# Predicting one edit: five engines made to run their instructions in the order of emission (hybrid decoder step, Trainium2)

## The chip, the core and the metric

The kernel runs on one NeuronCore of a Trainium2 chip, all of whose five engines it uses: TensorE (matmuls and transposes), VectorE, ScalarE, GpSimd and SyncE (which only issues the DMA transfers). Each engine runs its own list of instructions in the order of that list; an instruction waits for its operands at the head of the list, and the ones behind it wait with it. The metric is the device time of one execution in microseconds. Times are medians of several executions; the profile is of one more execution.

## The reference, cut to what matters

Two layers of a hybrid decoder over 1104 tokens (16 learned meta tokens and 1024 of a prompt, and 8 sequences of 8 sampled tokens), model width 1024, feed-forward width 2816. Three token mixers (gated DeltaNet with 4 heads, Mamba-2 with 4 heads, sliding-window attention with sinks) read one common input projection, and one output projection reads all three.

```python
def trunk_layer(x, pos, lw, states, front_pad, chunk, attend):
    m, new_states = hybrid_mixer(rmsnorm(x, lw['g_pre_mix']), pos, lw, states, front_pad, chunk, attend)
    x = x + rmsnorm(m, lw['g_post_mix'])
    gate, up = jnp.split(rmsnorm(x, lw['g_pre_ffn']) @ lw['w_ffn_in'], 2, axis=-1)
    x = x + rmsnorm((jax.nn.silu(gate) * up) @ lw['w_ffn_out'], lw['g_post_ffn'])
    return x, new_states
```

Inside the DeltaNet mixer a state is carried from block to block of the sequence, so its steps are a chain that can't be cut:

```python
    def step(s, inp):
        u_c, w_c, attn_c, qd_c, kd_c, gl_c = inp
        v_new = u_c - jnp.einsum('bhcd,bhde->bhce', w_c, s)
        o_c = jnp.einsum('bhcd,bhde->bhce', qd_c, s) + jnp.einsum('bhij,bhje->bhie', attn_c, v_new)
        s = s * gl_c[..., None, None] + jnp.einsum('bhcd,bhce->bhde', kd_c, v_new)
        return s, o_c
```

## The kernel before, in words

Tiles. The 1104 tokens are nine tiles of 128 tokens (the last has 80; `NT`, `tsz`). For full precision every weight slab comes from memory as float32 (`raw`) and is split into a high and a low float16 half (`wsp`): a ScalarE activation makes the high half, a VectorE `scalar_tensor_tensor` the low half. The activations are split in the same way (`xn`, `mixed`, `hsp`). A product is three float16 matmuls, accumulated in PSUM.

Stages of a layer. (1) Norm and transposition of the tokens into `xn`; input projections, attention, and the gates. (2) The DeltaNet and Mamba columns of the input projection, each followed by its short convolution (`conv_post`, tiles `R` and `u`), the preparation of each block of 128 tokens (`dn_inv`, `dn_prep`) and the chain over the blocks (`dn_chain`: `ps_ch`, `r`, `y`, `S`). (3) The output projection, from `mixed` into PSUM `pd`, then per tile the post-norm, the residual sum `xt`, the next norm and the transposes of `m` (`out_post`, line 2026). For the last three tiles (`NPT`) the part of the first three heads is computed early and parked in DRAM. (4) The feed-forward's input projection into `hid` and `hsp`, in a form with seven products in place of eight (`FSEQ`, `combos`, `hid_sums`). (5) The feed-forward's output projection with the post-norm `ffn_post`, which also makes the next layer's `xn`.

Who sets the order. The source is a set of generators (`dense`, `loader`, `dn_chain`, `out_post` and others), each of which emits some instructions and then yields a condition. The class `Plan` (line 116) chooses which goes on: it keeps a clock for each engine (`clk`, for T, V, S, G, D: TensorE, VectorE, ScalarE, GpSimd and the DMA queue of SyncE), adds the modelled duration of every emitted instruction (`note`, with `HOP` and `RATE`), and takes the generator of the lowest priority number that can go on without TensorE waiting. Its result is one list of instructions, in order of emission. All engine calls go through `Plan.engine` (line 206); its inner call stands at line 214, which is why every row of the profile bears L214, and rows are told apart by tile names.

The list of emission isn't yet the order on the engines. The framework's tile scheduler takes it, knows every data dependency, and puts each engine's instructions into an order by its own estimate of when each is ready; of several that are ready the first emitted goes first. So an instruction emitted later can stand ahead of one emitted earlier on the same engine, if the earlier one isn't expected to be ready. That order is fixed when the kernel is built.

Places that the steps below touch. The head of the program (lines 2108 to 2132) emits the loads in the order: first token tile, constants, gains, weight slabs 0 and 1, second token tile, slab 2, third token tile, slab 3; `first_load` (line 541) emits each slab's split at once, and all four stand before the first tile's square on ScalarE. In `dense` the output projection of a tile waits for all its inputs at once:

```python
                yield (tuple(("mix", l, h, i) for h in range(4)) + (("ssm", l, i), ("swa", l, i))
                       + tuple(wo if i == 0 else ()))
```

and after the nine tiles comes `yield (("ffn", l),)`, before the first feed-forward matmul is emitted. The buffers: 23 large ones in rotation (`NG`), two for raw slabs, three for split slabs, two PSUM banks for `pd` and six more for the short matmuls (`ps_tr`, `ps_inv`, `ps_ch`, `ps_o`).

Of the kernel before, what the change touches and what calls it, by code (L numbers as in the profile page):

```python
# [110 lines left out]

NG = 23
NOW = -1.0


class Plan:
# [38 lines left out]
    def note(self, k, name, out, ins, acc, slow=False):  # L155
# [40 lines left out]
        if k != "D" or out.space != DRAM:  # L196
# [6 lines left out]
                L.append(b + (e + self.HOP[k],))  # L203
            self.last = max(self.last, e + self.HOP[k])

    def engine(self, eng, k):
        plan = self

        class E:
            def __getattr__(self, name):  # L210
                f = getattr(eng, name)

                def call(*a, **kw):
                    r = f(*a, **kw)  # L214
                    aps = [x for x in list(a) + [v for n, v in kw.items() if n not in ("out", "accum_out")]
                           if isinstance(x, bass.AP)]
                    out = kw.get("out")
                    if out is None:
                        out, aps = aps[0], aps[1:]
                    plan.note(k, name, out, aps, [kw["accum_out"]] if "accum_out" in kw else [],  # L220
                              kw.get("op") is ALU.pow)
                    return r

                return call

        return E()

    def mark(self, *keys):
        for key in keys:
            self.done[key] = self.last  # L230
# [5 lines left out]
    def run(self, *until):  # L236

        done = self.done
        while not until or any(k not in done for k in until):
# [31 lines left out]
            best[1], best[2] = self.last, None  # L271
            if r == NOW:
                best[1] = 0.0
# [8 lines left out]
def build(tc, A, depth=DEPTH):  # L282
    nc = tc.nc
    P = Plan()
    V, S, G, T, DQ = (P.engine(e, k) for e, k in ((nc.vector, "V"), (nc.scalar, "S"), (nc.gpsimd, "G"),
                                                 (nc.tensor, "T"), (nc.sync, "D")))
    dma = DQ.dma_start
    mark, done = P.mark, P.done
    es = ExitStack()
# [8 lines left out]
    def act(out, in_, func=AF.Copy, **k):  # L298
        S.activation(out=out, in_=in_, func=func, **k)
# [4 lines left out]
    def tt(out, a, b, op):  # L304

        n = 1
        for x in out.shape[1:]:
            n *= x
        t = {k: max(P.clk[k], P.clk["T"]) + P.RATE[k][0] * n for k in "VG"}
        (V if t["V"] <= t["G"] else G).tensor_tensor(out, a, b, op=op)  # L310
# [42 lines left out]
    def PS(tag):  # L353
        n = {"tr": 1, "inv": 2, "ch": 1, "o": 2}[tag]
        t = psm.tile([128, 512], F32, tag=tag, bufs=n, name="ps_" + tag)
        P.take(tag, n, t)
        return t
# [31 lines left out]
    def later(key, fn, n=0):  # L389

        def g():
            yield (key,)
            fn()
            free(n)
            mark((key, "st"))
        P.add(0, g())

# [13 lines left out]
    def load7(my, key, src):  # L411
# [11 lines left out]
        for k in range(4):  # L423
# [5 lines left out]
            def put(o, x):  # L429
                yield P.clk["V"]  # L430
                act(w[:, o, :512], x, scale=WS)
                stt(w[:, o, 512:], x, WS, w[:, o, :512], MUL, SUB)
# [20 lines left out]
            mark(key + (k,))  # L453
            yield NOW

# [6 lines left out]
    def loader():  # L462
        while True:
# [31 lines left out]
            if key[0] == "w2" and key[2] == 0:  # L495
# [3 lines left out]
                split[0] += 1  # L499
                yield NOW  # L500
                continue
# [29 lines left out]
            mark(key)  # L531
            yield NOW

# [52 lines left out]
    def norm_t(xt, C, i, gb, dst, xs, tag, halves=False):  # L586
# [6 lines left out]
        for hf in range(2):  # L593
# [13 lines left out]
            V.tensor_tensor(lo, pc, hi, op=SUB)  # L607
            yield NOW if hf == 0 else None

# [19 lines left out]
    def dense_ws(p, w, xn, g):  # L629

        g0, gn = g
        for kt in range(8):
            mm3(p[:, :gn], w[:, 0, kt * 128:(kt + 1) * 128], w[:, 1, kt * 128:(kt + 1) * 128],
                xn[:, kt, 0, g0:g0 + gn], xn[:, kt, 1, g0:g0 + gn], kt == 0, kt == 7)
            if kt < 7:
                yield NOW

# [1622 lines left out]
def make(arrays, depth=DEPTH):  # L2260
    import concourse.bacc as bacc

    nc = bacc.Bacc("TRN2", target_bir_lowering=False, num_devices=1)
    A = {n: nc.dram_tensor(n, a.shape, mybir.dt.from_np(a.dtype), kind="ExternalInput").ap()
         for n, a in arrays.items()}
    for n, s in OUTS.items():
        A[n] = nc.dram_tensor(n, s, F32, kind="ExternalOutput").ap()
    with tile.TileContext(nc) as tc:
        build(tc, A, depth)
    return nc  # L2270
# [9 lines left out]
```

## Time and profile before

| | us |
|---|---|
| median of 3 executions | 2900.02 |
| lowest, highest | 2899.88, 2901.44 |
| the profiled execution | 2895.58 |
| its span in the trace | 2893.5 |

Mean granted clock of TensorE in the profiled execution: 0.981 of full speed. The rows of the views stand in a section of their own below. How to read them: times are microseconds; PE is TensorE's matmuls, PEld its weight loads, DVE is VectorE, ACT ScalarE, POOL GpSimd, SP SyncE. In a timeline each row is a run of like instructions: start, busy time, engine, operation, output<-input tiles, and how many; the bracket gives how long the engine stood idle just before and what ended that. Matmuls are pipelined, so their records overlap by some tenths of a microsecond.

### The profile page before, as it was taken

To read this page: it belongs to the slowest core of one execution; us is meant where nothing else is said; L and a number is where in the kernel's file an instruction comes from. 1 tells how busy PE (TensorE), PEld (TensorE's weight loads), DVE (VectorE), ACT (ScalarE), POOL (GpSimd) and SP (SyncE) were. 2 spreads that over 40 slices of the span, in tenths; PEclk is the share of its full clock that TensorE was granted. 3 is DMA by queue.
4 is the path that set the end of the run, shared out by engine and by line. 5 is a ranking of instruction groups with operands and counts; after the bars stand their busy time and mean duration, and the time that the engine had idled before them with its cause. 6 is when DMAs were issued, how large, how long until landed. Compare 5 with 4: busy or idle time off the path is not lost. (4 is left out here: it accounts for less than half of the span.)

```text
span 2893.5 us, 50019 instructions
## 1 busy us (share of the span) xinstructions
PE 2743.2 (95%) x19662; PEld 1909.5 (66%) x19662; DVE 1933.3 (67%) x3614; ACT 1288.4 (45%) x3015; POOL 813.1 (28%) x1124
## 2 busy tenths in 40 slices
PE   6999999999799999999899999999998999999997
PEld 3766677664588888744348676777646888886443
DVE  5557667655757676767865676666457666766776
ACT  5435456554423333433544455655543333334342
POOL 2204523313543333200260062223136233231011
PEclk8999999999899999999999999999999999999998
DMA  5011110132301111242431111001222111113333
GB/s 183 31 60 37 57 38 31 38 104 89 109 30 59 53 51 59 96 120 68 163 128 34 50 47 46 31 31 56 86 103 87 50 54 59 52 52 110 106 115 124
DMA packets 74092, 209.79 MB, mean 73 GB/s; under 512 B 13360, under 2 KB 24816, under 8 KB 73824
## 3 DMA queue, kind: packets, MB, share of 16 engines
q1 hardware_dynamic: 73856, 206.59, 21.8%
q8 instruction: 154, 2.52, 0.4%
q14 instruction: 82, 0.67, 0.1%
HBM read 175.49 MB, written 33.04 MB: 72 GB/s over the span
## 5 line engine op out<-in xcount | busy, mean ns | idle before, releaser
L214 PEld LDWEIGHTS <-wsp 128*128 128x128 f16 x10704 | 1044.1, 99 | 305.7 <-issue 12.9
L214 PE MATMUL pd<-xn,wsp 128*128 128x336 f16 (+3 forms) x4512 | 737.7, 311 | 3.4 <-DVE a L214 3.1
L214 DVE SCALAR_TENSOR_TENSOR wsp<-raw,wsp 128x512 f16<-128x512 f32 (+2 forms) x414 | 404.8, 986 | 196.3 <-ACT wsp L214 193.5
L214 ACT ACTIVATE wsp<-raw 128x512 f16<-128x512 f32 (+2 forms) x414 | 311.0, 763 | 393.5 <-DVE raw L214 145.9
L214 PEld LDWEIGHTS <-hsp 128*128 128x128 f16 x1848 | 182.1, 99 | 242.0 <-issue 30.2
L214 PE MATMUL pd<-wsp,hsp 128*128 128x512 f16 x924 | 232.6, 385 | 17.1 <-ACT wsp L214 11.8
L214 PE MATMUL ps_o<-wsp,hsp 128*128 128x512 f16 x924 | 230.7, 383 | 0.5 <-DVE m L214 0.5
L214 PE MATMUL pd<-wsp,mixed 128*128 128x512 f16 (+1 forms) x864 | 212.0, 384 | 5.8 <-DVE m L214 5.8
L214 POOL TENSOR_SCALAR rqy<-ss 128x1 f32<-128x1 f32 (+1 forms) x72 | 56.1, 779 | 551.1 <-ACT jk L214 407.6
L214 DVE SCALAR_TENSOR_TENSOR u<-R,lp_cw,u 128x512 f32<-128x512 f32 x216 | 180.0, 869 | 4.3 <-ACT u L214 3.4
L214 ACT ACTIVATE hsp<-hid 128x512 f16<-128x512 f32 x154 | 89.8, 620 | 180.4 <-PE ps_o L214 143.7
L214 PE MATMUL pd<-wsp,xn 128*128 128x512 f16 (+3 forms) x864 | 161.2, 338 | 6.0 <-ACT wsp L214 3.4
L214 PE MATMUL ps_o<-xn,wsp 128*128 128x256 f16 (+1 forms) x1296 | 165.1, 285 | 0.0
L214 POOL TENSOR_TENSOR raw<-raw 128x512 f32<-128x512 f32 x74 | 95.5, 1292 | 241.9 <-DVE raw L214 208.4
L214 PE MATMUL ps_inv<-xn,wsp 128*128 128x256 f16 (+1 forms) x1248 | 154.0, 281 | 0.8 <-DVE a L214 0.8
L214 POOL TENSOR_TENSOR U<-U,hid 128x256 f32<-128x256 f32 (+1 forms) x114 | 80.3, 733 | 239.3 <-ACT hid L214 239.3
L214 PEld LDWEIGHTS <-mixed 128*128 128x128 f16 (+1 forms) x864 | 84.4, 101 | 82.4 <-issue 11.3
L214 DVE TENSOR_TENSOR hsp<-hid,hsp 128x512 f16<-128x512 f32 x154 | 101.4, 684 | 43.3 <-ACT hsp L214 43.3
L214 PEld LDWEIGHTS <-xn 128*128 128x128 f16 (+1 forms) x864 | 87.4, 103 | 55.9 <-issue 10.7
L214 PE MATMUL ps_ch<-xn,wsp 128*128 128x296 f16 x456 | 109.2, 289 | 0.0
L214 PE MATMUL ps_tr<-xn,wsp 128*128 128x256 f16 x456 | 108.6, 273 | 0.0
L214 DVE TENSOR_TENSOR W<-ps_inv,c 128x512 f16<-128x512 f32 (+1 forms) x120 | 71.0, 595 | 46.3 <-PE ps_inv L214 45.4
(496 smaller groups left out, 4738.9 us busy)
## 6 DMA issues: line engine op xcount, KB each, us to landing
raw<-wfi SPq DMA_DIRECT2D x88, 512.0 KB, 3.5
raw<-wfo SPq DMA_DIRECT2D x70, 512.0 KB, 3.7
raw<-wf SPq DMA_DIRECT2D x44, 512.0 KB, 3.3
xd<-xt SPq DMA_DIRECT2D x24, 512.0 KB, 2.9
xt<-xd SPq DMA_DIRECT2D x24, 512.0 KB, 5.7
xt<-x SPq DMA_DIRECT2D x16, 512.0 KB, 6.1
raw<-wo SPq DMA_DIRECT2D x16, 512.0 KB, 3.4
tcx<-wfo SPq DMA_DIRECT2D x10, 512.0 KB, 3.7
```

The lines of the kernel that those rows point to most:

```text
L214: r = f(*a, **kw)
```

## The change

Every instruction on the five engines gets an ordering edge to the instruction emitted before it on the same engine. The edge is for the tile scheduler alone: it says "not ahead of that one" and adds no wait for that one's end. Nothing is added to the work, taken from it or given another shape; which buffer of a rotation an instruction uses, and for whom it waits, can differ as the order does.

```diff
+PINNED = "TVSGD"
...
+    def keep(self, k, ins):
+
+        return self.pin(ins) if k in PINNED else ins
...
                 def call(*a, **kw):
-                    r = f(*a, **kw)
+                    r = plan.keep(k, f(*a, **kw))
...
     P = Plan()
+    P.pin = tc.keep_in_program_order
```

## Rows read from the trace of the kernel before

**Rows 1.** Top of the page: the span, then busy time (share, instructions) of each engine.
```profile
span 2893.5 us, 50019 instructions
...
PE 2743.2 (95%) x19662; PEld 1909.5 (66%) x19662; DVE 1933.3 (67%) x3614; ACT 1288.4 (45%) x3015; POOL 813.1 (28%) x1124
```

**Rows 2.** Table by stage: stretch, its length, busy time of engines, clock, DMA share, GB/s.
```profile
core 0: us, PE busy (x) PEld busy (x) DVE busy (x) ACT busy (x) POOL busy (x), PEclk, DMA share, GB/s
0.00:61.40 61.40, 41.15 (x212) 22.61 (x212) 32.41 (x55) 31.38 (x68) 16.16 (x35) 0.92 0.54 186
...
240.00:640.00 400.00, 377.80 (x2992) 278.57 (x2990) 268.83 (x565) 229.03 (x597) 138.09 (x208) 0.99 0.15 50
640.00:684.00 44.00, 41.08 (x259) 25.92 (x257) 19.79 (x57) 18.30 (x66) 11.18 (x18) 1.00 0.18 60
...
752.00:791.00 39.00, 29.72 (x222) 24.04 (x221) 31.93 (x35) 15.98 (x30) 25.19 (x26) 0.85 0.36 119
791.00:1390.00 599.00, 598.90 (x4406) 433.30 (x4405) 416.25 (x767) 221.67 (x457) 144.71 (x176) 1.00 0.22 69
1390.00:1470.00 80.00, 67.92 (x314) 30.93 (x313) 70.40 (x82) 40.26 (x66) 23.19 (x26) 0.96 0.56 179
...
1660.00:2064.00 404.00, 382.04 (x3021) 281.75 (x3020) 271.48 (x569) 230.66 (x599) 138.07 (x208) 0.99 0.15 50
...
2815.00:2893.00 78.00, 57.83 (x245) 24.75 (x243) 56.42 (x65) 23.38 (x36) 15.06 (x12) 0.89 0.38 129
```

**Rows 3.** Waits of TensorE, 240 to 640: waiting tile <- releaser, sum, times, longest.
```profile
PE ps_ch L214 <- ACT qs L214: 6.7, 3, 3.2
PE ps_ch L214 <- DVE lt L214: 3.9, 2, 2.0
```

**Rows 4.** Timeline of all engines, 502 to 513, without the weight loads.
```profile
503.22 2.00 PE L214 MATMUL ps_ch<-Sb,kq 128*128 128x128 f32 x16
...
505.69 3.62 DVE L214 SCALAR_TENSOR_TENSOR u<-R,lp_cw,u 128x616 f32<-128x616 f32 x3
...
509.23 0.33 DVE L214 SCALAR_TENSOR_TENSOR r<-ps_ch,nE,prep 64x128 f32<-64x128 f32 x1
...
509.93 0.39 PE L214 MATMUL ps_ch<-S,ck 128*16 128x128 f32 x2 [3.20 <-ACT qs L214]
```

**Rows 5.** The end of the chain, 646.5 to 683.5, all instructions (columns as rows 2).
```profile
646.50:683.50 37.00, 34.08 (x207) 21.53 (x206) 16.29 (x49) 15.24 (x57) 10.27 (x15) 1.00 0.19 64
```

**Rows 6.** The same stretch, instructions on `pd` alone: PE, DVE, ACT busy.
```profile
646.50:683.50 37.00, 15.97 (x56) 0.00 (x0) 1.83 (x4) 1.00 0.19 64
```

**Rows 7.** Timeline of TensorE, 745 to 791.
```profile
744.62 2.10 PE L214 MATMUL pd<-wsp,mixed 128*128 128x512 f16 x9
748.85 0.63 PE L214 MATMUL ps_tr<-c,m 128*128 128x128 f32 x4 [2.12 <-DVE m L214]
...
752.01 1.75 PE L214 MATMUL ps_o<-xn,wsp 128*128 128x256 f16 x8
...
760.42 3.19 PE L214 MATMUL ps_o<-xn,wsp 128*128 128x256 f16 x14
763.41 0.75 PE L214 MATMUL ps_tr<-c,m 128*128 128x128 f32 x4
```

**Rows 8.** Timeline of all engines, 750 to 771: steps of the norm chains.
```profile
755.06 3.36 DVE L214 SCALAR_TENSOR_TENSOR xt<-m,rqy,xt 128x1024 f32<-128x1024 f32 x1 [2.10 <-POOL rqy L214]
...
760.90 1.06 ACT L214 ACTIVATE xn<-xt 128x1024 f16<-128x1024 f32 x1
760.94 0.55 POOL L214 TENSOR_TENSOR rqy<-rqy,mhalf 128x1 f32<-128x1 f32 x1
...
761.52 1.28 DVE L214 SCALAR_TENSOR_TENSOR m<-xt,rqy,gpf 128x1024 f32<-128x1024 f32 x1 [0.72 <-POOL rqy L214]
```

**Rows 9.** Timeline of VectorE, 1396 to 1412: one of the products.
```profile
1400.35 1.22 DVE L214 TENSOR_TENSOR m<-m,gb 128x1024 f32<-128x1024 f32 x1
```

**Rows 10.** Timeline of ScalarE, 0 to 45: the fourth weight split.
```profile
23.37 1.06 ACT L214 ACTIVATE wsp<-raw 128x1024 f16<-128x1024 f32 x1
```

**Rows 11.** Timeline of TensorE, 0 to 45: its first instructions.
```profile
8.48 1.11 PE L214 MATMUL ps_tr<-c,xt 128*128 128x128 f32 x4 [8.48 <-DVE xt L214]
```

## The prediction, made before the changed kernel was built

> **What bounds the kernel now.** I read the page first. TensorE is busy in 2743.2 of the 2893.5 us, so at most 150 us of the span can be saved by any order, and any loss must show as new idle time on that engine [rows 1]. The table by stage says where the 150 us lie [rows 2]. One stretch of the feed-forward input projection fills TensorE: 598.90 of 599.00 us. The idle time sits at the head (61.40 against 41.15), in the token mixers of each layer (400.00 against 377.80, so 22.2 us), at the end of the DeltaNet chain (44.00 against 41.08), between out-projection and feed-forward (39.00 against 29.72, so 9.3 us), in the feed-forward's output (80.00 against 67.92, with VectorE busy 70.40) and in the tail. The second layer repeats the first, one row of it stands for that. So the change is priced by these stages. In the mixers I then read the waits of TensorE [rows 3]: it stands mostly before the short matmuls of the DeltaNet chain, which need a ScalarE or VectorE result.
>
> **What the change does to an engine.** No instruction is added or removed. Both kernels issue on each engine in one fixed order; before, a scheduler chose it and let ready work overtake, after, it is the order of emission, which the planner chose. The instructions carry the number of their emission. Outside the longest run in order stand 964 of the 18,392 matmuls, 1,234 of the 3,614 VectorE, 614 of the 2,759 ScalarE, 214 of the 1,121 GpSimd and 97 of the 487 SyncE instructions; most are within 200 numbers of their place. An overtaker either filled a hole or made something more urgent late. Pinning gives back the second kind and loses the first. I took each stage for itself.
>
> **Mixers, gain.** The rows show the second kind. A matmul group into `ps_ch` ends at 505.22. The VectorE step `r` that reads it runs at 509.23, behind three convolution steps of 3.62 us in all; the next chain matmul starts at 509.93 after 3.20 us of idle TensorE [rows 4]. In the source the `r` is emitted before those three. I followed the larger gaps of the 22.2 us back in the same way, and in some nine tenths of that time the releasing step had been ready behind a later-emitted one. I take three quarters as given back, 15 us, as an estimate. Against it: convolutions that were early will now be late, and the in-order ScalarE and VectorE wait for each other; 8 us of new idle time, an estimate from about a third of what stands there today. Net -7 us a layer, bounds -18 and +15.
>
> **Chain end, loss.** In 646.5 to 683.5 the chain of the last head runs, and the only other work for TensorE is the out-projection of tiles 0 to 5, for the heads that are done. The scheduler moved 54 of these matmuls (`pd<-wsp,mixed`) into the holes of the chain: of 34.08 us of TensorE time in 37.00, they are 15.97 as the profile counts overlapping records [rows 5, 6]. In the source `dense` waits for all four heads of a tile, and in the emission these matmuls all come after the chain. Their real price is the pipelined rate, 2.10 us for 9, 0.23 us each [rows 7]: 54 x 0.23 = 12.5 us that move behind the chain. The chain, freed of them, should be some 2 us shorter. Net +10 us a layer, bounds +4 (chain quicker by half of them) and +13.
>
> **Out-projection to feed-forward.** Here feed-forward matmuls (`ps_o<-xn,wsp`, at 752.01 and 760.42 for 1.75 and 3.19 us) run before the transposes `ps_tr<-c,m` of the last tiles at 763.41 [rows 7]. In the source, nine tiles' out-projection and all nine norms come first. TensorE then waits out the norm chain of a tile: eviction, square on ScalarE 1.06 (plus its accumulator), reciprocal root on GpSimd, `xt` on VectorE, square 1.06, root 0.55 and its step before, `m` 1.28 [rows 8]. That is 7 to 8 us, and up to 9 where `xt` meets GpSimd's product, as its 3.36 us do. Walking the emission by hand with these durations I get two stalls of 7.5 and 8.4 us and 2.3 us of small ones, 18.2 instead of 9.3. Before 752 the strict order saves some 4 us, among them the 2.12 us at 748.85 [rows 7], whose norm was overtaken. Net +5 a layer, bounds -3 and +12.
>
> **Feed-forward output.** VectorE is nearly full there. Now the products `m<-m,gb` of 1.22 us stand between the steps that split the weights [rows 9]; in the source they come later, which gives time back. But a split is a ScalarE step and then a VectorE step, and in strict order VectorE waits where it used to take something else. I take +3 a layer, bounds -5 and +15 (two bubbles of about a microsecond for each of the slab pairs).
>
> **Head.** ScalarE's fourth weight split runs at 23.37 today, and TensorE starts at 8.48 [rows 10, 11]. In the source the four splits stand before the first tile's square, so TensorE starts when the fourth slab has landed and a norm is done: about 23, an estimate from the issue of these transfers moving up a few microseconds. The 41.15 us of work up to 61.40 [rows 2] then end near 65 if nothing else is late: +4, bounds -2 and +12.
>
> **At nothing.** Feed-forward input: TensorE has no idle time to lose, but every one of the queues could stall it; VectorE is at 416.25 of 599.00 [rows 2], which leaves cover. Bound +6 a layer. SyncE: DMA share is 0.15 to 0.22 in the long stages [rows 2], so a transfer that is issued some places later is covered; without that cover a slab would stall TensorE by its landing, so I keep +-3. Sum: 2 x (-7 + 10 + 5 + 3) + 4 = +26 us. The profiled run took 2895.58 us, 2.1 more than its span and 4.4 under the median; so 2921.6 for such a run and 2926 for the median.
>
> **A clock rule.** TensorE's granted clock is 1.00 at the chain end and 0.85 in the stretch after it that has the stalls [rows 2]. The second means that part of it ran at 1.2 instead of 2.4 GHz, after idle time. If the chain end without its fillers fell to that 0.85, and the next 39 us to 0.75, the cost would be 37 x 0.15 + 39 x 0.10 = 9.5 us a layer, 19 in all: 2945. The Trainium skill, "TensorE: Matmul & The Clock Gate", section "What's actually happening", says that the engine's default is the halved clock and that only recent activity lifts it. By that rule the loss is larger than the moved matmuls alone; the 0.85 agrees, and no row shows the chain end without fillers. I count it as a rival.
>
> **Rivals.** (1) Faster: overtaking on VectorE is what makes the idle time. Place: the mixers' chain steps. If these stalls go to under 5 us a layer (-18), the chain end costs only 5, out-projection evens out, feed-forward output gives 2 and the head 2, the sum is 2 x -15 - 2 = -32: 2868. For it: rows 4 repeat all over the mixers. Against it: the holes at chain end are shown. It decides if the mixers gain over 16 us a layer. Chance 0.31. (2) The halved clock, 2945, chance 0.10. (3) New waits everywhere: putting today's matmuls into source order and leaving their producers' ends where they are gives 144 us more idle time (worked out over all 19,662 records [rows 1]), of which at most 85 were delayed by overtaken producers. If a half of that is not recovered the loss is about 100: 3000. Chance 0.08. (4) The gains of the mixers (-13) and the losses (+8, +5) cancel: 2900, chance 0.11.
>
> **How the numbers follow.** The forecast, slower by 6 to 60 us, has 0.40. Under and over 0.2%, 6 us, is what a measurement of this kernel can tell from no change. Faster 0.31, same 0.11, slower 0.40 + 0.10 + 0.08 = 0.58. The forecast's own range is 2906 to 2955. Most of rival 1 must be inside: the range is 2868 to 2980, and it leaves out the far half of rivals 1 and 3.
>
> **What would show it.** Right: idle TensorE time before `ps_ch` in the mixers falls by half; between 646 and 684 no `pd<-wsp,mixed` stand among the chain's matmuls and TensorE is busy about half the time; two stalls of 7 to 8 us before `ps_tr<-c,m`; the first matmul after 20 us. Wrong: fillers that the planner itself emitted into the chain end, or a feed-forward input stage with more than 6 us of idle time, which would be a queue that I held to be covered.

## The result and the profile after

The changed kernel takes 3025.09 us (median of 4 executions, 3023.55 to 3028.07), the one before 2899.95 in the same series: 1.0434 times as long, 95% interval 1.0421 to 1.0447. That is 125 us more where +26 was forecast, and above the range, whose upper end was 2980.

The top of the page after, as in rows 1:

```profile
span 3022.1 us, 49957 instructions
...
PE 2780.8 (92%) x19662; PEld 1938.9 (64%) x19662; DVE 1972.1 (65%) x3614; ACT 1282.4 (42%) x3015; POOL 812.4 (27%) x1124
```

The same 19,662 matmul records now take 37.6 us more of TensorE's time, and the span is 128.6 us longer; so 91 us are new idle time, and 38 us are the same work taking longer, at a mean granted clock of 0.958 where it had 0.981. The table by stage of the kernel after shows both (columns as in rows 2, the first number after the stretch and its length being TensorE's busy time; the stretches are about those of rows 2, found again by emission numbers, and so lie elsewhere on the time axis):

```profile
229.00:601.00 372.00, 350.35 (x2746) 265.77 (x2745) 254.95 (x549) 209.90 (x553) 140.92 (x204) 0.96 0.12 42
...
640.00:687.30 47.30, 33.89 (x154) 23.64 (x154) 18.55 (x55) 15.42 (x57) 10.11 (x15) 0.73 0.14 44
...
759.70:817.50 57.80, 35.18 (x232) 27.47 (x232) 42.39 (x52) 23.66 (x43) 30.85 (x33) 0.76 0.34 110
817.50:1425.00 607.50, 599.46 (x4406) 433.15 (x4404) 420.48 (x749) 208.63 (x443) 141.20 (x169) 1.00 0.21 67
1425.00:1535.00 110.00, 86.03 (x376) 38.92 (x374) 84.48 (x96) 49.33 (x80) 21.44 (x35) 0.91 0.42 141
```

The chain end (second line) has lost its fillers: the granted clock is 0.73, a mean of stretches at 2.4 and at 1.2 GHz, where rows 2 have 1.00. The stretch of the last tiles' norms (third line) has 22.6 us of idle TensorE in 57.8. The feed-forward output (last line) is 110 us long, with VectorE busy 77% of it; rows 2, over its densest 80 us, have 88%.

The numbers of emission are the same in both kernels, so a ledger can be made: for each stage, the end of the last matmul whose number lies below the stage's last one, minus the same for the stage ahead. Each column is one execution. The runs on which the argument rests are in it; of others that leave the source's order alone, single stages are quoted below (us; layer 1, then layer 2; "V" is VectorE, "T" TensorE, "FFN" the feed-forward; the runs are told below; "V in mixers" has the pins in the head too):

| stage | before | all pinned | T alone | all but T | all but V | V in mixers | V after mixers |
|---|---|---|---|---|---|---|---|
| head and attention in | 230.3 | 219.9 | 230.6 | 220.2 | 222.1 | 234.0 | 229.9 |
| mixers, first part | 193.1 | 183.6 | 192.9 | 179.8 | 192.7 | 180.5 | 194.8 |
| mixers, second part | 222.6 | 235.3 | 242.2 | 222.8 | 239.2 | 222.4 | 223.7 |
| chain end | 37.6 | 45.6 | 44.0 | 40.3 | 47.6 | 39.1 | 41.2 |
| out-projection, first FFN columns | 137.4 | 163.5 | 159.7 | 147.4 | 163.6 | 137.8 | 146.0 |
| FFN in | 498.9 | 507.6 | 500.2 | 508.3 | 503.0 | 498.9 | 506.8 |
| FFN out | 164.6 | 186.0 | 172.4 | 185.2 | 177.8 | 164.8 | 178.4 |
| layer 2: attention in | 167.8 | 166.6 | 165.6 | 169.5 | 166.9 | 167.8 | 165.2 |
| mixers, first part | 195.4 | 184.3 | 195.2 | 181.7 | 201.5 | 182.7 | 197.1 |
| mixers, second part | 222.0 | 235.0 | 246.6 | 222.1 | 238.6 | 224.1 | 222.6 |
| chain end | 37.4 | 50.6 | 48.9 | 39.8 | 47.3 | 37.5 | 38.0 |
| out-projection | 139.5 | 166.8 | 162.5 | 161.2 | 165.9 | 139.6 | 157.4 |
| FFN in | 499.4 | 510.2 | 500.8 | 508.1 | 505.3 | 499.4 | 503.6 |
| FFN out | 136.4 | 152.9 | 139.1 | 151.9 | 144.4 | 136.1 | 149.0 |

Read it by columns: what the change gave (the head 10, the first part of the mixers 10 and 11) and what it took (13 a layer in the second part of the mixers, 8 and 13 at the chain ends, 26 and 27 in the out-projection, 9 and 11 in the feed-forward input, 21 and 17 in its output).

The waits of TensorE in the whole kernel after, longest kinds (waiting tile <- releaser, sum, times, longest):

```profile
PE ps_tr L219 <- DVE m L219: 72.8, 21, 11.1
PE pd L219 <- ACT wsp L219: 26.3, 9, 5.4
```

The first stood at 31.2 us before, the second at 15.2: the transposes behind the norms, and the weight slabs of the feed-forward output. The two stalls of the forecast's pair are seen in TensorE's timeline after:

```profile
762.21 1.46 PE L219 MATMUL pd<-wsp,mixed 128*128 128x512 f16 x6
772.40 1.09 PE L219 MATMUL ps_tr<-c,m 128*128 128x128 f32 x4 [8.73 <-DVE m L219]
...
785.43 1.09 PE L219 MATMUL ps_tr<-c,m 128*128 128x128 f32 x4 [8.53 <-DVE m L219]
```

### The profile page after: what moved, and what is told of

The parts are those of the page before. It is cut to its first block, busy times and chain, and to the rows that moved or that the text cites. A ratio compares the mean times of both kernels' runs of the same rounds, so it can differ in the third digit from the quotient of the medians.

```text
span 3022.1 us, 49957 instructions
## 1 busy us (share of the span) xinstructions
PE 2780.8 (92%) x19662; PEld 1938.9 (64%) x19662; DVE 1972.1 (65%) x3614; ACT 1282.4 (42%) x3015; POOL 812.4 (27%) x1124
## 5 line engine op out<-in xcount | busy, mean ns | idle before, releaser
L219 PE MATMUL pd<-xn,wsp 128*128 128x336 f16 (+3 forms) x4512 | 728.1, 310 | 6.6 <-ACT xn L219 3.5
L219 DVE SCALAR_TENSOR_TENSOR wsp<-raw,wsp 128x512 f16<-128x512 f32 (+2 forms) x414 | 378.0, 924 | 205.1 <-ACT wsp L219 202.9
L219 POOL TENSOR_SCALAR rqy<-ss 128x1 f32<-128x1 f32 (+1 forms) x72 | 37.5, 521 | 641.8 <-ACT jk L219 444.5
L219 PE MATMUL pd<-wsp,xn 128*128 128x512 f16 (+3 forms) x864 | 154.7, 332 | 0.0
L219 DVE SCALAR_TENSOR_TENSOR hid<-a,hid 128x256 f32<-128x256 f32 (+2 forms) x190 | 85.2, 465 | 40.6 <-ACT a L219 38.0
```

Source lines behind the costliest of these rows:

```text
L219: r = plan.keep(k, f(*a, **kw))
```

## The experiments

The theory after the result was A: what TensorE loses are matmuls that filled holes, and now stand behind what waits. The rival was B: the orders of the other engines make new waits. Differences are against the kernel before as timed with each run. Two executions of such a run lie up to 15 us apart, so I draw nothing from differences under some 8 us unless the ledger shows their place.

**1. Which engine's order: TensorE alone, all but TensorE.**

```diff
-PINNED = "TVSGD"
+PINNED = "T"        # first run
+PINNED = "VSGD"     # second run
```

> Only TensorE in the order of emission, the other four engines ordered by the scheduler as before. The changed kernel lost 125 us: by common instruction numbers -10 in the head, 0 in the mixers, +32 at the two chain ends, +58 between the out-projections and the feed-forwards (first feed-forward columns included), +50 in the feed-forward outputs. Theory A (TensorE's own order: matmuls that used to fill holes now stand behind what waits): chain ends and out-projections lose the same here, 32 + 58, the outputs little: 2985, 2960 to 3010. Theory B (the other engines' orders make the new waits): 2900 to 2930.

> TensorE ordered by the scheduler, the other four in the order of emission. Theory A: the matmuls fill the holes at the chain ends and out-projections again, the outputs of the feed-forward stay slow (waits on ScalarE's and VectorE's weight splits): 2940, 2915 to 2965. Theory B: 3000 to 3025, nearly all of the loss stays.

Measured: 3018.0 (+124) with TensorE alone, outside both answers, and 2957.6 (+64) with all but TensorE, inside A's range (2915 to 2965). TensorE's order alone costs as much as all five, and the other four without it half as much. The two don't add up to 125, so the losses share places. The ledger parts them. TensorE's own order costs the second part of the mixers (+20 and +25), the chain ends and most of the out-projection's loss (22 and 23 of 26 and 27). The other four orders give the head and the mixers their gain, and cost the feed-forward: its input 9 us a layer, its output 21 and 16. They also cost the out-projection 10 and 22 without TensorE's. So A and B are both there, mostly each in stages of its own, and in the out-projection either is enough for much of the loss.

**2. The DMA queue free.**

```diff
-PINNED = "TVSGD"
+PINNED = "TVSG"
```

> As the changed kernel, but SyncE's DMA queue is ordered by the scheduler. If loads that stand behind stores in the queue delay the norm chains (the store of a token tile waits for its last step, the next tile's load is issued after it), 10 to 25 us come back: 3000 to 3015. If the loads are early enough anyway, nothing moves: 3025 within 6.

Measured: 3014.3 (+121). By the time itself that lies just inside the first answer, by the difference (+121 against +125) it is the second: nothing moves. The ledger has 4 us less in each feed-forward output, and 9 more in the head, where TensorE's first matmul comes at 28.41 in place of 19.47. The queue's order is no term of the loss.

**3. VectorE free.**

```diff
-PINNED = "TVSGD"
+PINNED = "TSGD"
```

> As the changed kernel, but VectorE is ordered by the scheduler. The theory says that overtaking on VectorE was what cost the first half of the mixers and what filled the bubbles of the feed-forward output. So mixers: the gain of 10 us a layer goes, +20; feed-forward input and output: 10 + 20 us a layer come back, -55; sum 2990. If the stages don't hang on VectorE but on ScalarE's or the queue's order, the mixers keep their gain and the outputs stay slow: 3015 to 3030.

Measured: 3031.5 (+132), outside the first answer and just above the second. The total hides that the mechanism did show: the mixers' gain goes (192.7 and 201.5, where all pinned gives 183.6 and 184.3), and the feed-forward gets back 5 a layer in its input and 8 in its output. What I had wrong is the size of the second part: TensorE, still pinned, holds the rest.

**4. VectorE's order alone, in one place at a time.** Here the pins are switched with the stage, and only VectorE has them (`PINNED = "V"`):

```diff
+    on = True              # in the second run False
...
-        return self.pin(ins) if k in PINNED else ins
+        return self.pin(ins) if self.on and k in PINNED else ins
...
             mark(("gains", l))
+            P.on = False       # second run: True
...
         sub.close()
+        P.on = True            # second run: False
         sub = ExitStack()
         L.ssp = pool("ssm", 1, stack=sub)
```

> VectorE alone in the order of emission, and only where the faster mixed version has its pins (head, first layer's attention, mixers of both layers); every other engine ordered by the scheduler. If overtaking on VectorE is what the mixers lost, their 10 to 12 us a layer come here too, the head's gain (which went where the DMA queue was free) does not: 2876 to 2882. If it takes all four orders, 2890 to 2900.

> VectorE alone in the order of emission, and only from the out-projection to the end of the next layer's attention (out-projection, feed-forward in and out); every other engine ordered by the scheduler. With TensorE free and the other four pinned these stages lost 52 and 46 us. If VectorE's order makes these waits, 2950 to 2990. If they come from ScalarE's, GpSimd's or the queue's order, or only from orders that don't fit each other, 2899 to 2915.

Measured: 2872.4 (-25; ratio 0.9912, interval 0.9895 to 0.9928) with VectorE pinned in the mixers, and 2961.0 (+64; 1.0222, 1.0196 to 1.0247) with it pinned after them. The first goes a little beyond its first answer (2876 to 2882), the second lies in its first. One engine's order is thus the gain in one stage and most of the feed-forward's loss in another. In VectorE's timeline of the first of the two the step `r` of rows 4 runs when its matmul is done, and convolution steps like those that stood ahead of it come after:

```profile
499.97 0.34 DVE L220 SCALAR_TENSOR_TENSOR r<-ps_ch,nE,prep 64x128 f32<-64x128 f32 x1 [2.27 <-PE ps_ch L220]
...
505.69 0.74 DVE L220 SCALAR_TENSOR_TENSOR u<-R,lp_cw,u 128x512 f32<-128x512 f32 x1
...
508.59 0.84 DVE L220 SCALAR_TENSOR_TENSOR u<-R,lp_cw,u 128x616 f32<-128x616 f32 x1
```

and of TensorE's waits in the mixers (240 to 600) the longest kind is a quarter of the one in rows 3:

```profile
PE ps_ch L220 <- ACT qs L220: 1.7, 3, 1.1
```

In the second of the two, VectorE's timeline in the feed-forward output has a fixed pattern, which the changed kernel shows with the same times:

```profile
1420.29 1.22 DVE L220 TENSOR_TENSOR raw<-tcx,raw 128x1024 f32<-128x1024 f32 x1
1422.63 1.22 DVE L220 SCALAR_TENSOR_TENSOR wsp<-raw,wsp 128x1024 f16<-128x1024 f32 x1 [1.12 <-ACT wsp L220]
1423.77 0.68 DVE L220 TENSOR_TENSOR hsp<-hid,hsp 128x512 f16<-128x512 f32 x1
1424.37 1.22 DVE L220 TENSOR_TENSOR raw<-raw,tcx 128x1024 f32<-128x1024 f32 x1
1426.71 1.23 DVE L220 SCALAR_TENSOR_TENSOR wsp<-raw,wsp 128x1024 f16<-128x1024 f32 x1 [1.12 <-ACT wsp L220]
```

The source emits a slab's subtraction, ScalarE's half and VectorE's half back to back. In that order VectorE stands idle 1.12 us for ScalarE's half, for each slab. Before, the next slab's subtraction or a norm's product ran there [rows 9]. From late in layer 1's feed-forward input to the end of its output, VectorE's waits of this kind sum to 12.8 us in the changed kernel and to 3.5 before.

**5. Is that bubble the loss of the feed-forward output?** Two tries. One lets the planner emit other work inside the pair, everything pinned; the other takes the version with VectorE pinned after the mixers and lets two kinds of steps move ahead again.

```diff
             act(w[:, 0, :n], x, scale=WS)
+            if key[0] == "w2":
+                yield None                     # first try
             stt(w[:, 1, :n], x, WS, w[:, 0, :n], MUL, SUB)
...
+                    P.on, on = "", P.on        # second try, here and around hsp's
                     V.tensor_tensor(raw, *((x, raw) if key[2] == 7 else (raw, x)), op=SUB)
+                    P.on = on
```

> As the changed kernel, all engines in order of emission; but in the feed-forward output's weight slabs the planner may emit other work between the ScalarE half of a split and the VectorE half that needs it. If the bubbles of 1.12 us of VectorE before each second half are what makes this stage 21 and 16 us longer, most of it comes back: 2993 to 3003. If the order of the slabs against the sums of hid sets it, or the clock, 3015 to 3028.

> As the version that pins VectorE alone from the out-projection on (+64 us), but two kinds of its VectorE steps in the feed-forward output may move ahead again: the subtraction that prepares a weight slab (raw) and the low halves of hid (hsp). So one of them can run in the 1.12 us in which VectorE waits for a split's ScalarE half. If that bubble is what VectorE's order costs there, the outputs go from 178 and 149 us to 166 and 138: 2899 + 64 - 23 = 2940, 2930 to 2945. If it is the place of the norm products or the slabs' order, 2955 to 2965.

Measured: 3041.7 (+143, so 17 worse than the changed kernel) and 2951.9 (+52, 11 better than the version that it is made from, against 23 expected). VectorE in the first try:

```profile
1454.88 1.22 DVE L219 SCALAR_TENSOR_TENSOR wsp<-raw,wsp 128x1024 f16<-128x1024 f32 x1
1456.61 0.69 DVE L219 TENSOR_TENSOR hsp<-hid,hsp 128x512 f16<-128x512 f32 x1 [0.51 <-ACT hsp L219]
1460.08 1.23 DVE L219 TENSOR_TENSOR raw<-raw,tcx 128x1024 f32<-128x1024 f32 x1 [2.78 <-DMA raw<-wfo]
```

The bubble of 1.12 us is gone, and a wait of 2.4 to 3.3 us for the next slab's load has come in its place. There are two raw buffers, a load can start when a split has freed one, and in strict order what stands behind the subtraction stands with it. So the try failed by a wait that it made itself. In the second try the ledger has 173.7 and 144.3 for the outputs, with 178.4 and 149.0 where VectorE is all pinned and 164.6 and 136.4 before. Freeing these two kinds of steps thus gives back about a third of what VectorE's order costs there. That try has waits for loads of its own, so the bubble's exact share is not shown; which other steps make the rest I have not parted.

**6. Fillers at the chain end.** The planner, read out while it emits, gives the reason why they are missing. All 23 large buffers are taken from the gains' load on. `dense` can't pass its `room(2)` for the first tile until the last chain frees four, and by the planner's own clock TensorE idles 19.0 us there (the trace has 13.5, at a lower clock). In two steps I emitted a full tile's matmuls ahead of that condition; the second doesn't wait for the last head either:

```diff
             for i in range(NT):
                 C = tsz(i)
+                ps = []
+                if i not in part:
+                    yield (tuple(("mix", l, h, i) for h in range(3)) + (("ssm", l, i), ("swa", l, i))
+                           + tuple(wo if i == 0 else ()))      # first step: range(4)
+                    for hf in range(2):
+                        ps.append(pd())                        # first step: all eight slabs here
+                        yield from dense_tok(ps[hf], mx, wo[hf * 4:hf * 4 + 4], i, 512, (0, 1, 2, 4, 5, 6, 7),
+                                             last=False)
+                        yield NOW
+                    yield (("mix", l, 3, i),)
+                    for hf in range(2):
+                        yield from dense_tok(ps[hf], mx, wo[hf * 4:hf * 4 + 4], i, 512, (3,), first=False)
+                        yield NOW
                 yield room(2)
                 hold(2)
```

> As the changed kernel, all engines in order of emission; but dense emits the two halves' matmuls of a full tile's out-projection ahead of the condition room(2), the wait for two of the 23 large buffers, which the planner's own account grants only when the last head's chain is done. So the planner can emit some 48 matmuls into the chain end. If that room is what keeps the fillers out, and the halved clock comes from the missing work, the two chain ends get back most of their 32 us: 2995 to 3005. If the fillers were not the cause, or block the chain's own matmuls, 3020 to 3030.

> As the changed kernel, all engines in order of emission; but a full tile's out-projection for the first three heads and the other mixers (seven of eight slabs) is emitted without waiting for the last head or for the two buffers, the eighth slab when that head is there. So 48 of its matmuls stand among the last chain's, as many as the scheduler put there (44), where the earlier try got 30 in. If the missing fillers are the loss of this stretch, 11 us of work a layer move and the clock stays up: 2995 to 3003. If the norm chains and rooms of the tiles set the end of the out-projection whatever stands in the chain, 3015 to 3027.

Measured: 3022.8 (+129) and 3010.6 (+113). The first, as its second answer said, put 30 matmuls ahead of the chain's last step and gained nothing; the second, between its two answers, put 48 there, about as many as the scheduler, and gained about 12 us. The ledger charges 8 and 13 us to the chain ends, and the moved matmuls some 10 us a layer to the out-projection. The stage table of the second:

```profile
640.00:675.00 35.00, 30.57 (x199) 21.69 (x197) 13.27 (x44) 12.81 (x51) 8.21 (x13) 0.97 0.10 34
675.00:755.00 80.00, 64.12 (x280) 28.75 (x277) 44.47 (x51) 28.83 (x51) 23.89 (x30) 0.87 0.31 112
```

and a kind of wait that the changed kernel doesn't have in this stretch:

```profile
PE pd L219 <- ACT m L219: 8.4, 5, 3.2
```

Up to 675 the clock is back at 0.97; from the chain's first matmul to its last it is 0.89, where the changed kernel has 0.74:

```profile
640.50:681.40 40.90, 32.42 (x200) 21.96 (x199) 17.65 (x52) 13.72 (x54) 10.11 (x15) 0.89 0.14 45
```

The chain's last step is 3 us earlier, with 48 more matmuls in it; in layer 2 the chain takes 40.8 us in place of 47.1. The first step had the clock at 0.89 as well, but its chain took 46.1 us: there the fillers stood in the chain's way. In the out-projection TensorE then has less to do and meets what stands behind: an eviction per tile and the norms. So part of what is filled in ahead is given back right behind it.

**7. Fillers in the out-projection.** By the planner's clock TensorE idles 22.8 us there as well (the trace: 27.9): the last tiles wait for two of the 23 buffers, which a norm two tiles ahead frees, and the feed-forward is behind them in the same generator. I gave the loop over the tiles a generator of its own.

```diff
-            for i in range(NT):
-                ...                       # the loop, with what frees wo and mixed
+            P.add(8, outproj(L, part, wo, mx))
```

> As the changed kernel, all engines in order of emission; but the out-projection's loop is a generator of its own, so that the planner can emit the feed-forward's first matmuls beside the last tiles, which it holds back otherwise until the ninth. The run with fillers at the chain end gained nothing by the end of the out-projection, so its end is set by the tiles' norm chains and the two-buffer rooms, and TensorE's stalls there can only be filled with feed-forward work. If that is so, the stalls of 8.7 and 8.5 us and the halved clock of that stretch go: 15 to 20 us a layer, 2985 to 2995. If the rooms that the feed-forward takes delay the last tiles, 3015 to 3030.

Measured: 3018.0 (+119; two executions 15 us apart, the profile of the slower one), in the second answer. The stalls of 8.73 and 8.53 us are gone, and shorter ones stand at the transposes and the tiles' matmuls:

```profile
777.09 0.81 PE L219 MATMUL pd<-wsp,mixed 128*128 128x512 f16 x3 [2.79 <-DVE m L219]
...
791.32 1.09 PE L219 MATMUL ps_tr<-c,m 128*128 128x128 f32 x4 [4.87 <-DVE m L219]
```

This execution was 4.4 us late at the chain's last step already, so I count from there. The last tile's matmuls end after 108.1 us where the changed kernel has 105.6, and the feed-forward's first combined operand is used after 186.2, there after 188.3; in layer 2 it is 108.0 against 106.3 and 186.1 against 194.1. Feed-forward work was moved into the holes, and the tiles' chains were moved back by it: 17 us of stalls gone bring 2 and 8 us. So the end of this stretch is set for the most part by nine norm chains, of which the buffers let two go on at a time, and less by TensorE's work. Both edits together were not run.

**8. The clock.** Useless matmuls on constants ahead of the last three tiles' transposes, everything pinned.

```diff
-            p = v4(PS("tr" if hf == 0 else "ch"))
+            pt = PS("tr" if hf == 0 else "ch")
+            p = v4(pt)
+            if halves and i > 5 and hf == 0:
+                for _ in range(16):
+                    P.keep("T", nc.tensor.matmul(pt, lhsT=c16[:, :128], rhs=c16[:, 128:640], start=True, stop=True))
```

> As the changed kernel, with useless work added: 16 matmuls of 512 columns on constants into the transposes' own bank ahead of the transposes of the last three tiles in each out-projection, where TensorE stands idle 21 us a layer; the real transposes overwrite it. 2 x 3 x 16 x 0.22 = 21 us of work that fits into the holes. If the halved clock of this stretch (0.77) is part of the loss, it goes to 0.9 or more and the stretch is 4 to 7 us a layer shorter in spite of the added work: 3010 to 3017. If the clock costs nothing there because the norm chains set the end, 3024 to 3032.

Measured: 3031.8 (+135), in the second answer. The stage table of this run, and the third of the added groups in TensorE's timeline:

```profile
640.00:687.30 47.30, 34.45 (x147) 24.43 (x147) 16.38 (x50) 14.29 (x55) 10.10 (x15) 0.63 0.13 42
...
759.70:817.50 57.80, 41.76 (x259) 28.10 (x257) 38.93 (x46) 21.94 (x40) 28.77 (x31) 0.85 0.35 117
...
806.01 3.61 PE L605 MATMUL ps_tr<-c 128*128 128x512 f16 x16 [1.17 <-DVE xn L219]
```

The clock of the last stretch rose from 0.76 to 0.85 and nothing ended earlier: from the chain's last step to the last transposes it is 133.4 us, with 130.2 without the added work. The 3.2 us more are the third group's own: only two of the three found a hole, and the third stands right ahead of the last transposes. Up to the last tile but one the times agree within half a microsecond. There the lower clock follows from the waits and is not what they cost, as far as a rise to 0.85 can tell. That holds for this stretch; for the second part of the mixers (clock 0.85 from 403.7 to 471.7 in the changed kernel, 1.00 before) I have no such run, and at the chain ends the rows below say otherwise.

**9. What the ledger leads to.** Three versions with pins only where they paid and TensorE free: VectorE, ScalarE, GpSimd and the queue up to the mixers' end and off after it; the queue alone in the head with VectorE alone in the mixers; and the four in the head with VectorE alone in the mixers. The switch is the one of experiment 4; the second and third have a string of engines in place of the flag:

```diff
-        return self.pin(ins) if k in PINNED else ins
+        return self.pin(ins) if k in self.on else ins
```

> VectorE, ScalarE, GpSimd and SyncE in the order of emission in the head, the attention of the first layer and the DeltaNet and Mamba mixers of both; TensorE ordered by the scheduler everywhere; from the gains' load before the last chain on, and in the attention of the second layer, no pins. By the ledger of the run with TensorE free: head -7, attention -3, first half of the mixers -13 and -14, second half 0, the rest as before the change. So 37 us faster than before, 2857, if the stages are independent. If the gain in the mixers is only borrowed (the scheduler's order later makes up for it at the chain end, where fillers are then missing), 2885 to 2900.

> SyncE's DMA queue alone in the order of emission in the head and the first layer's attention, VectorE alone in the mixers of both layers, nothing else. If the order of the loads is what made the head faster (the changed kernel needs 220 us to the end of the attention, the one before 230, the one with a free queue 229), 8 to 10 us come here, and 24 from the mixers: 2862 to 2868, the fastest of all. If the head needs ScalarE's order too (the four splits ahead of the first square), only the mixers' gain: 2873 to 2877.

> VectorE, ScalarE, GpSimd and SyncE's queue in the order of emission in the head and the first layer's attention, VectorE alone in the mixers of both layers, TensorE free everywhere, nothing pinned after the mixers. If the head needs the four together, its 8 us (222 in place of 230 at the end of the attention) add to the mixers' 27: 2858 to 2864. If head and mixers don't add up, as 2869 and 2870 for the two earlier versions: 2867 to 2872.

Measured: 2870.3 (-29; ratio 0.9907, 0.9891 to 0.9924), 2869.2 (-30; 0.9897, 0.9880 to 0.9913) and 2872.4 (-29; 0.9906, 0.9889 to 0.9922). None of the three lies in its first answer. All three beat the kernel before by 1%, and can't be told apart, nor from VectorE alone in the mixers (experiment 4, ratio 0.9912): no gain beyond that one is shown. After the mixers their stages are those of the kernel before within 2 us (137.3, 498.9, 164.9 for the first of them), so the mixers' gain isn't given back later. The head and the mixers don't add up as I had expected: to the end of the first layer's mixers' first part the three need 405.3, 409.4 and 410.2 us where before had 423.4. The four orders in the head, without the same pins in the mixers, didn't give what they give with them. What made the head faster in the changed kernel is therefore not settled; a free queue loses it by a later start (experiment 2), and the queue alone doesn't make it.

## Why the prediction was wrong

**The direction and the two mechanisms** were right: overtaking gave in the holes and cost on VectorE. The sum was made too small by a factor of five. By its steps:

- *Mixers, -7 a layer.* Measured +3 and +2. The gain came as reasoned, but smaller: 10 and 11 in the first part, for which I had 15 (experiment 4 gives 13 for VectorE's order alone). The step that failed is "8 us of new idle time": the second part of the mixers costs 13 a layer by all pins and 20 and 25 by TensorE's alone. I had looked for new waits on ScalarE and VectorE, and it is TensorE's own order. Of the 13 in layer 1 only 5 are idle time; 7 are TensorE taking longer for the same work, at a clock of 0.93 where it had 0.99, and the forecast had no clock in this term. Whether that clock or the waits set the length there is open.
- *Chain end, +10.* Measured +8 and +13, but near by luck. The +10 was 12.5 us of work moved behind the chain, less 2 us by which the chain should be quicker. The fillers did go, but the moved work is charged to the out-projection in this ledger, and the chain itself became 8 and 10 us longer. The step that failed is "the chain, freed of them, should be some 2 us shorter". The chain from its first matmul to its last, layer 1 and layer 2 after, and layer 1 before (layer 2 before is the same):

```profile
639.50:684.30 44.80, 31.29 (x153) 22.88 (x152) 16.98 (x52) 13.49 (x54) 10.11 (x15) 0.74 0.13 40
2127.90:2175.00 47.10, 33.66 (x153) 24.54 (x152) 17.13 (x52) 13.52 (x54) 10.12 (x15) 0.66 0.12 38
...
646.60:683.50 36.90, 33.98 (x206) 21.48 (x205) 16.29 (x49) 15.24 (x57) 10.27 (x15) 1.00 0.19 64
```

The two chain ends after have the same matmuls in the same order and the same idle time, 13.5 and 13.4 us, and differ by 2.3 us with the clock, 0.74 and 0.66. The four chain ends without fillers in experiment 1's first run and in experiment 3 lie near the same line: 43.3 us at 0.78, 43.8 at 0.74, 45.4 at 0.70, 46.8 at 0.66. Carried on to 1.00 the first two give some 37 us, an estimate. So nearly all of the chain's 8 and 10 us go with the halved clock, which I had left to rival 2.

- *Out-projection, +5.* Measured +26 and +27, the largest miss. The two stalls were forecast at 7.5 and 8.4 and came at 8.73 and 8.53. Wrong was what I set against them: I let the strict order save 4 us before them, while the same waits at the earlier tiles went from 8.8 to 6.9 us in all; and a third stall, of 3.78 us, brought the idle time of the last tiles to 22.6 where I had 18.2. Some 10 of the 26 are the chain end's in this ledger, since the matmuls that no longer run there run here (45 more records between the chain's last step and the feed-forward's first combined operand, at 0.23). The two together were forecast at +15 and measured +34 and +41. In layer 1, before and after:

```profile
646.20:821.20 175.00, 153.96 (x964) 99.46 (x963) 108.77 (x161) 70.51 (x157) 84.61 (x90) 0.95 0.26 86
...
639.00:848.10 209.10, 167.66 (x964) 108.16 (x963) 101.86 (x157) 69.20 (x154) 68.57 (x79) 0.86 0.23 75
```

Of the 34, 20 are idle time and 14 are the same 964 matmul records taking longer at the lower clock, for which the forecast had nothing.

- *Feed-forward output, +3.* Measured +21 and +17. I had the bubble ("about a microsecond for each of the slab pairs") as the bound of +15, and took a fifth of it because hoisted products of 1.22 us would give time back. Before, such products stood in those very bubbles, so moving them gave little back. The bound was nearer than the value, but the bubble is not the whole loss: VectorE's order makes 14 and 13 of it, of which freeing two kinds of steps gave back 5 (experiment 5). What makes the rest is open.
- *Feed-forward input at nothing, bound +6.* Measured +9 and +11. The text named this as its own way to be wrong. It is the four other orders, VectorE's alone for 8 and 4 of it: with TensorE alone pinned it is +1.
- *Head, +4.* Measured -10 with the attention behind it. The start was late as forecast, if less so: ScalarE's splits came first, and TensorE began at 19.47, where I had about 23.

```profile
15.08 1.06 ACT L219 ACTIVATE wsp<-raw 128x1024 f16<-128x1024 f32 x1 [1.50 <-DMA raw<-wtA]
```

That is the fourth split, at 23.37 before [rows 10]: the loads of the slabs moved up, and afterwards TensorE has 6.6 us of idle time up to 66.9, where it had 17.7 up to 71.0 after its early start at 8.48 [rows 11]. I had counted the later start and not the holes that the early start had. But the two only balance: over the head and the attention TensorE idles 26.4 us, and 26.2 before. The 10 us are in its busy time, 193.7 against 204.2 for the same matmuls, at a granted clock of 1.00 against 0.94. The clock alone isn't the cause either: with TensorE alone pinned it is 0.99 there, and the stage is as long as before, with 31.0 us idle.

**The rivals.** The third, "new waits everywhere" at 3000, came nearest, and its first-order number of +144 us was the better forecast: I took 85 of it as recoverable since the producers had themselves been overtaken. The planner's list explains why it wasn't. Its own clock leaves TensorE idle for 198 us, of which 178 lie in the four stages that lost (by layer: second part of the mixers 16 and 16, chain end 19 and 19, out-projection 23 and 26, feed-forward output 35 and 24), and the changed kernel idles 207 us by the same measure, from TensorE's first matmul to its last. Its buffers are counted, and a step that has no room holds all that its generator would emit behind it. The scheduler before had no such rule and filled in what was ready. The second rival, the halved clock, was right as to the fact (0.73 and 0.70 in the chain ends' stretch, where I had put 0.85). It had a price at the chain ends, whose 8 and 10 us come near the 19 that it had for both layers with the stretches behind them, and none that showed in the last tiles' stretch (experiment 8). The Trainium skill, "TensorE: Matmul & The Clock Gate", section "What's actually happening", says that only recent activity lifts the clock: the 0.74 without fillers and the 0.89 with them (experiment 6), from the chain's first matmul to its last, agree.

## What to carry to other kernels

An order that a planner wrote is as good as its account: before pinning it, look where the planner itself leaves the busiest engine idle, since whoever reordered it was filling those places. Price an overtaking step by what it stood in front of: if that was ready, the engine's order is worth pinning there (VectorE in the mixers, -25 us); if nothing was, the step filled a bubble and was free (VectorE in the feed-forward output). And pin by engine and stage: here one engine's order gained 1% in one stage and lost 2% in the next.

## What the runs showed of the hardware that I had not expected

The same matmuls took 37.6 us more of TensorE's time in the changed kernel, as the granted clock fell in stretches with idle time spread through them: 0.73 and 0.70 at the chain ends, 0.85 early in the second part of the mixers. What that costs depends on the place. In the last tiles' stretch, 48 added matmuls a layer lifted the clock from 0.76 to 0.85 and shortened nothing: there the waits set the end. At the chain ends the chain's own matmuls are the path, and the same ones took 36.9 us at 1.00, with other work among them, 44.8 at 0.74 and 47.1 at 0.66. Work that fills the holes of such a chain can make the chain itself shorter (experiment 6, layer 2: 47.1 to 40.8 us).
